# The first two output pairs of a hybrid decoder layer, from a plain and a seven-product multiplication to two interleaved seven-product ones

## Chip, cores and metric

The kernel runs on one core of a Trainium2 chip, as one program. The metric is the device time of one execution in microseconds (us). The kernel before was timed in three runs: median 869.21 us, from 868.64 to 869.86.

## What is computed

The reference is one layer of a hybrid decoder over 2048 rows of width 1024, with 16 learned rows ahead of them, in float32:

```python
hn = rms_norm(h, norm_g)
proj = jnp.einsum('bld,de->ble', hn, w_in)              # 1024 -> 8 groups of 512
cx, cb, cc, cg, q, k, v, rg = jnp.split(proj, N_PROJ, axis=-1)
conv_out = short_conv_branch(cx, cb, cc, conv_w) * jax.nn.silu(cg)
ret_out = head_group_norm(retention_chunkwise(rotary(q), rotary(k), v), g) * jax.nn.silu(rg)
mixed = jnp.concatenate([conv_out, ret_out], axis=-1)
h = h + jnp.einsum('ble,ed->bld', mixed, w_out)         # the output projection
return rms_norm(h, final_g)
```

The change is in the last product, `mixed @ w_out`, a 2048 x 1024 by 1024 x 1024 multiplication, and in the sum and the norm behind it.

## The kernel before

**Numbers in two parts.** Every float32 operand of a large product is split into a high part, which ScalarE (ACT) casts to the matmul type, and a low part, which VectorE (DVE) makes as the operand less its high part (`split`, L112 and L113). One 128 x 512 piece of a product is then three matmuls: low by high, high by low, high by high. On the weight side (stationary) the two parts are the tiles `wh` and `wl`, on the moving side `mh` and `ml`. The stationary tiles live in a ring of three (RING), the moving ones of a whole matrix stay in SBUF: `mh20` to `mh23` are the four 128-row pieces of moving operand 2.

**Seven products.** A 2 x 2 product of blocks is done in seven block products in place of eight, with sums of blocks as operands (Winograd's form). On the stationary side GpSimd (POOL) makes the sums for each pair (`stationary`, four additions and subtractions of 128 x 512). The moving side has seven operands, m0 to m6, four blocks or sums of blocks each. A block product is 12 matmuls (four pieces by three), so seven products are 84 matmuls; `quad` (L236) issues them, with a ScalarE copy of some PSUM banks, and `take` adds up the results. `quad_plain` (L293) does the eight plain products in 96 matmuls, from four stationary parts that it keeps as moving-type tiles, and needs m0, m1, m5 and a plain fourth block m7 alone.

**Stages.** The sequence is done in two halves of 1024 rows; in each half eight units (four retention heads, four convolution groups) project, mix and store 128 columns of `mixed` to DRAM. Behind them the output stage takes `mixed` back in eight pairs of 128-row tiles (`output`, pairs 0 to 7): load four `ra` tiles of `mixed`, multiply by w_out, add the rows of `x` (the `yo` tiles), square and sum on ScalarE, normalise, store. The sums of w_out blocks (m2, m3, m4 and m6, that is `SUMS`) were made in earlier units and lie in DRAM (`sums_w`); those of m3 and m4 are loaded ahead during the last convolution group into the tiles `held`, the others come through the tiles `t`.

**The first pair before.** Pair 0 runs plain, so that it needs no sums; while it runs, m2 and m6, and then m3 and m4, are split. Pairs 1 to 7 run in seven products. In pair 1 the addition of a copied bank to `yo` is on VectorE, in the later pairs on GpSimd.

**What sets the order.** The program is written in Python order, but a scheduler places instructions on each engine by its own estimate of readiness. Each engine then runs its row of instructions strictly in that order: an instruction whose operand is late holds all behind it. All loads and stores named here are issued by SyncE's queue (SP).

## Time and profile before

| | us |
|---|---|
| median of three runs | 869.21 |
| the profiled execution, whole | 868.33 |
| its span, on which the times of the trace are counted | 866.5 |
| TensorE (PE) busy in the span | 855.4 |
| VectorE busy | 725.7 |
| ScalarE busy | 497.8 |
| GpSimd busy | 394.6 |

The trace counts from the start of the span. In it the last convolution group's fifth block product is issued until 697.85 us, the first matmul of the output stage starts at 697.85, and TensorE's last matmul is over some seven us before the span's end. A matmul's duration in a row (0.39 us) is longer than its share of the engine, since matmuls overlap; what one costs is the distance between starts. In a row of the timeline the columns are start, duration, engine, line, operation, tiles and count, and in brackets the idle time ahead and what ended it.

### The profile page before, as it was taken

The numbers are of one execution on the slowest core, as the hardware profiler recorded it, in microseconds if no ns is written. First come the engines' busy times: TensorE is split into PE (matmuls) and PEld (weight loads), VectorE is DVE, ScalarE is ACT, GpSimd is POOL, SyncE is SP. The second block draws the span as 40 slices with busy tenths as digits, with TensorE's granted clock in tenths as the row PEclk, the third lists the DMA queues.
The fourth block names the chain that finished last, engine by engine and source line by source line (L and its number), as shares of the span: only waits on it lengthen the run. The fifth ranks groups of instructions, "written<-read, shape, count | busy, mean of one in ns | idle before, by whom it ended". The sixth has DMA issues, their size and how long they took to land.

```text
span 866.5 us, 12699 instructions
## 1 busy us (share of the span) xinstructions
PE 855.4 (99%) x4216; PEld 705.1 (81%) x4216; DVE 725.7 (84%) x1194; ACT 497.8 (57%) x899; POOL 394.6 (46%) x286
## 2 busy tenths in 40 slices
PE   9999999999999999999999999999999999999996
PEld 6778888888787778788888888888888888788885
DVE  7899988888988977989789898988767799877663
ACT  8676548384755554948374757544333566545553
POOL 0662332423145554352242323354746555677773
PEclk9999999999999999999999999999999999999999
DMA  9724235454656633845264845646123584555431
GB/s 339 233 79 89 72 85 154 113 149 135 159 169 190 199 98 98 313 149 146 62 158 121 159 134 124 205 113 216 48 78 81 173 326 136 169 165 178 156 134 73
DMA packets 127218, 129.51 MB, mean 149 GB/s; under 512 B 58352, under 2 KB 75568, under 8 KB 127152
## 3 DMA queue, kind: packets, MB, share of 16 engines
q1 hardware_dynamic: 126576, 128.30, 50.0%
q8 instruction: 33, 0.54, 0.3%
q10 hardware_dynamic: 576, 0.40, 0.1%
q14 instruction: 33, 0.27, 0.1%
HBM read 90.91 MB, written 25.17 MB: 134 GB/s over the span
## 4 chain that ended last, share of the span: by engine, by line
PE 78%; DVE 6%; issue 1%; ACT 0%; POOL 0%; POOLq 0%; DVEq 0%
PE pj L236 66%; PE pj L293 5%; PE ms L831 1%; PE ms L820 1%; PE ms L830 1%; PE ms L807 1%; DVE wl L113 1%; PE ms L456 1%; DVE ml L113 1%; DVE ml L116 0%; DVE yo L121 0%; DVE yo L906 0%; DVE yo L941 0%; ACT n L407 0%; DVE tc L121 0%
## 5 line engine op out<-in xcount | busy, mean ns | idle before, releaser
L236 PE MATMUL pj<-mh,wl 128*128 128x512 f32 x1008 | 396.0, 393 | 1.3 <-DVE wl L113 0.7
L236 PE MATMUL pj<-mh,wh 128*128 128x512 f32 x1008 | 393.1, 390 | 0.0
L236 PE MATMUL pj<-ml,wh 128*128 128x512 f32 x1008 | 392.9, 390 | 0.0
L112 ACT CAST wh<-ra 128x512 fp32r<-128x512 f32 x216 | 133.9, 620 | 232.1 <-PE pj L236 193.6
L236 PEld LDWEIGHTS pj<-mh,wl 128*128 128x128 f32 x1008 | 189.3, 188 | 43.1 <-issue 1.5
L113 DVE TENSOR_TENSOR wl<-ra,wh 128x512 fp32r<-128x512 f32 x216 | 192.4, 893 | 36.6 <-ACT wh L112 35.2
L236 PEld LDWEIGHTS pj<-mh,wh 128*128 128x128 f32 x1008 | 189.3, 188 | 39.4
L236 PEld LDWEIGHTS pj<-ml,wh 128*128 128x128 f32 x1008 | 189.3, 188 | 38.1
L121 POOL TENSOR_TENSOR sa<-ra 128x512 f32<-128x512 f32 x36 | 54.1, 1504 | 108.8 <-DMA ra<-in_w_in 50.5
L124 POOL TENSOR_TENSOR ra<-sa,ra 128x512 f32<-128x512 f32 x36 | 51.3, 1424 | 81.8 <-DVE wl L113 79.6
L124 POOL TENSOR_TENSOR ra<-ra 128x512 f32<-128x512 f32 x36 | 59.1, 1641 | 59.2 <-PE ms L456 48.9
L151 POOL TENSOR_TENSOR ra<-ra 128x512 f32<-128x512 f32 x36 | 61.5, 1709 | 47.3 <-issue 35.2
L243 ACT COPY tc<-pj 128x512 f32<-128x512 f32 x108 | 62.6, 580 | 0.1
L293 PE MATMUL pj<-mh,mh 128*128 128x512 f32 x128 | 51.0, 401 | 0.6 <-ACT mh L115 0.6
L293 PE MATMUL pj<-mh,ml 128*128 128x512 f32 x128 | 50.0, 390 | 1.0 <-DVE ml L113 1.0
L293 PE MATMUL pj<-ml,mh 128*128 128x512 f32 x128 | 48.0, 391 | 0.0
L843 POOL TENSOR_TENSOR rp<-rs,neg_half 128x4 f32<-128x4 f32 x16 | 19.4, 1211 | 46.4 <-DVE rs L121 46.2
L596 POOL TENSOR_TENSOR c<-c,rr 128x512 f32<-128x512 f32 x14 | 25.7, 1834 | 22.2 <-DVE c L637 14.1
L906 DVE TENSOR_TENSOR yo<-pj,yo 128x512 f32<-128x512 f32 (+1 forms) x33 | 22.0, 671 | 15.9 <-PE pj L236 8.5
L917 POOL TENSOR_TENSOR z<-yo,final_g 128x512 f32<-128x512 f32 x16 | 26.8, 1674 | 18.6 <-DVE yo L906 18.6
L847 DVE TENSOR_SCALAR pm<-ms,mv,rp 128x128 f32<-128x128 f32 x64 | 21.9, 403 | 11.8 <-POOL rp L843 11.8
L112 ACT CAST wh<-sa 128x512 fp32r<-128x512 f32 x36 | 22.2, 618 | 16.0 <-PE pj L236 15.8
(153 smaller groups left out, 1223.2 us busy)
## 6 DMA issues: line engine op xcount, KB each, us to landing
ra<-in_w_in SPq DMA_DIRECT2D x126, 256.0 KB, 2.9
x<-in_xT SPq DMA_DIRECT2D x48, 256.0 KB, 5.0
w<-in_w_out SPq DMA_DIRECT2D x32, 256.0 KB, 4.7
ra<-mixed SPq DMA_DIRECT2D x32, 256.0 KB, 2.7
yo<-in_x SPq DMA_DIRECT2D x32, 256.0 KB, 4.6
ra<-in_x SPq DMA_DIRECT2D x16, 256.0 KB, 3.3
mixed<-c SPq DMA_DIRECT2D x16, 256.0 KB, 2.5
sums_x<-x SPq DMA_DIRECT2D x16, 256.0 KB, 2.8
```

The costliest lines, as they stand in the source:

```text
L112: nc.scalar.copy(out=hi, in_=src)
L113: lowered[0] = eng.tensor_tensor(out=lo, in0=src, in1=hi.bitcast(F32), op=ALU.subtract)
L121: eng.tensor_tensor(out=out, in0=a, in1=b, op=ALU.add)
L124: eng.tensor_tensor(out=out, in0=a, in1=b, op=ALU.subtract)
L151: summed[0] = nc.gpsimd.tensor_tensor(out=a12, in0=a12, in1=a11, op=ALU.subtract)
L236: nc.tensor.matmul(bank, a[:, ks], b, start=first and kt == 0 and n == 0, stop=kt == KH - 1 and n == 2, skip_group_check=not first,)
L243: copied[0] = nc.scalar.copy(out=c, in_=bank)
L293: nc.tensor.matmul(banks[i], a[:, ks], b, start=half + kt + n == 0, stop=half == 1 and kt == KH - 1 and n == 2,)
L596: eng.tensor_tensor(out=out, in0=a, in1=b, op=ALU.mult)
L847: nc.vector.tensor_scalar(out=y[:, cs], in0=o[:, cs], scalar1=mv[:, c, 0:1], scalar2=rp[:, c, :], op0=ALU.subtract, op1=ALU.mult,)
L906: last[0] = nc.vector.tensor_tensor(out=y[:, cs], in0=pp[:, cs], in1=y[:, cs], op=ALU.add)
L917: nc.gpsimd.tensor_tensor(out=ys[i][j], in0=y, in1=final_g[:, j * HB : (j + 1) * HB], op=ALU.mult)
```

## The change

The first two pairs no longer run one after the other. A new function `quads` runs them together: product 0 of pair 0, product 0 of pair 1, product 1 of pair 0 and so on, both in seven products, each with two PSUM banks. `stationary_in_turn` is a generator: it makes a pair's seven stationary operands one by one, in the order in which the products use them, with the same four GpSimd operations as `stationary`, but in place, without the tile `sa`; the operand of product 4 is written over that of product 3. `moving_in_turn` splits m0 and m1 first, and m2, m3, m4, m5, m6 between the products, in that order. The plain fourth block m7 is no longer made. The rows of `x` for both pairs are loaded behind the first product, the additions of copied banks to `yo` are all on GpSimd, and the norms of both pairs are written behind the last product.

```diff
-    lowered, fifth = [None], [None]
     def split(hi, lo, src, scale=None, eng=nc.vector):
         if scale is None:
             nc.scalar.copy(out=hi, in_=src)
-            lowered[0] = eng.tensor_tensor(out=lo, in0=src, in1=hi.bitcast(F32), op=ALU.subtract)
+            sub(eng, lo, src, hi.bitcast(F32))
             return
         nc.scalar.mul(hi, src, scale)
         nc.vector.scalar_tensor_tensor(
...
         sub(nc.gpsimd, a21, a11, a21)
         sub(nc.gpsimd, a11, s1, a11)
         summed[0] = nc.gpsimd.tensor_tensor(out=a12, in0=a12, in1=a11, op=ALU.subtract)
-        w += [parts(a) for a in (a11, s1, a21)]
-        fifth[0] = lowered[0]
-        return w + [parts(a) for a in (a12, a22)]
+        return w + [parts(a) for a in (a11, s1, a21, a12, a22)]
+    def stationary_in_turn(blocks):
+        a11, a12, a21, a22 = blocks
+        def parts(src):
+            hi = sb.tile([P, HB], F32R, name="wh", tag="wh", bufs=RING)
+            lo = sb.tile([P, HB], F32R, name="wl", tag="wl", bufs=RING)
+            split(hi, lo, src)
+            return hi, lo
+        yield parts(a11)
+        add(nc.gpsimd, a21, a21, a22)
+        sub(nc.gpsimd, a11, a21, a11)
+        yield parts(a12)
+        sub(nc.gpsimd, a12, a12, a11)
+        yield parts(a11)
+        yield parts(a21)
+        sub(nc.gpsimd, a21, a22, a11)
+        yield parts(a21)
+        yield parts(a12)
+        yield parts(a22)
     def operand(i, kt):
         slot = B12 if i == 7 else i
...
                     parts(m, BLOCK[half][j], kt, blocks[-1], scale(k) if scale else None)
                     after.get((j, k), lambda: None)()
         return m, blocks
+    def moving_in_turn(load, scale, sums):
+        m = [[] for _ in range(8)]
+        def blocks(half, j):
+            for kt in range(KH):
+                k = half * KH + kt
+                parts(m, BLOCK[half][j], kt, load(k, j), scale(k) if scale else None)
+        blocks(0, 0)
+        blocks(1, 0)
+        steps = [
+            lambda: sums(m, 1), lambda: sums(m, 0), lambda: sums(m, 2), lambda: blocks(1, 1), lambda: sums(m, 3),
+        ]
+        return m, steps
     def block_sums(b11, b12, b22, b21, t1, t3, f, g, eng=nc.vector):
...
         take(0, 1, zb, u2)
         product(6, xb, False)
         take(1, 0, xb, None)
...
+    def quads(ws, m, takes, between=()):
+        between = iter(between)
+        banks = [[None, None] for _ in ws]
+        copies = [None for _ in ws]
+        def product(n, i, bank, first):
+            wh, wl = next(ws[n])
+            for kt in range(KH):
+                ks = slice(kt * P, (kt + 1) * P)
+                mh, ml = m[i][kt]
+                for s, (a, b) in enumerate(((wl, mh), (wh, ml), (wh, mh))):
+                    nc.tensor.matmul(
+                        bank, a[:, ks], b, start=first and kt == 0 and s == 0, stop=kt == KH - 1 and s == 2,
+                        skip_group_check=not first,
+                    )
+        def copy(bank):
+            c = sb.tile([P, HB], F32, name="tc", tag="tc", bufs=COPIES)
+            copied[0] = nc.scalar.copy(out=c, in_=bank)
+            return c
+        for i in range(7):
+            for n, take in enumerate(takes):
+                if i < 2:
+                    banks[n][i] = ps_proj()
+                bank = banks[n][1 if i in (1, 3, 5) else 0]
+                product(n, i, bank, i in (0, 1, 3))
+                if i == 0:
+                    copies[n] = copy(bank)
+                elif i == 1:
+                    take(0, 0, bank, copies[n])
+                elif i == 2:
+                    copies[n] = [copy(bank)]
+                elif i == 3:
+                    copies[n].append(copy(bank))
+                elif i == 4:
+                    take(1, 1, bank, copies[n][1])
+                elif i == 5:
+                    take(0, 1, bank, copies[n][0])
+                else:
+                    take(1, 0, bank, None)
+            next(between, idle)()
...
-    def output(pair, m, final_g):
+    def output(pair, final_g):
...
-        for i in range(2):
-            for j in range(2):
-                y = gen("yo")[:, :HB]
-                row = (2 * pair + i) * P
-                nc.sync.dma_start(y, x[row : row + P, j * HB : (j + 1) * HB])
-                ys[i][j] = y
+        def fetch():
...
-                with tc.issue_after(fifth[0].ins) if pair == 1 and i + j == 0 else nullcontext():
-                    add(nc.vector if pair == 1 else nc.gpsimd, y, y, c)
+                add(nc.gpsimd, y, y, c)
...
-                if pair and i + j == 0:
+                if pair > 1 and i + j == 0:
...
-        if pair == 0:
-            w = plain_parts(loads)
-            prepared(m, sums_w, (1, 3))
-            quad_plain(w, m, take)
-            prepared(m, sums_w, (0, 2), held)
-        else:
-            quad(stationary(load_raw(loads)), m, take, (idle, idle, square))
-        for i in range(2):
...
+        def finish():
+            for i in range(2):
...
+        return loads, fetch, take, square, finish
...
-    m, b = moving(load_w_out)
+    m, in_turn = moving_in_turn(load_w_out, None, lambda m, n: prepared(m, sums_w, (n,), held))
     final_g = row_tile("final_g", 1)
     nc.sync.dma_start(final_g, t["final_g"].partition_broadcast(P))
-    for pair in range(SEQ // (2 * P)):
-        output(pair, m, final_g)
+    first_pairs = [output(pair, final_g) for pair in range(2)]
+    def behind_first(sums=in_turn[0]):
+        sums()
+        for _, fetch, *_ in first_pairs:
+            fetch()
+    quads(
+        [stationary_in_turn(load_raw(loads)) for loads, *_ in first_pairs], m, [take for _, _, take, *_ in first_pairs],
+        [behind_first] + in_turn[1:],
+    )
+    for *_, finish in first_pairs:
+        finish()
+    for pair in range(2, SEQ // (2 * P)):
+        loads, fetch, take, square, finish = output(pair, final_g)
+        fetch()
+        quad(stationary(load_raw(loads)), m, take, (idle, idle, square))
+        finish()
```

Up to the last convolution group all five engines have the same rows of instructions as before. The places from which the rows differ are these.

TensorE at the end of the last convolution group, before. `pj` are PSUM banks; L236 is `quad`, L293 `quad_plain`. Product 5 of the convolution (`mh50` by `wl_6911`) stands behind a first part of pair 0:

```order
L293 MATMUL pj_7205<-mh03_7046,mh30_7135 128x512
L293 MATMUL pj_7205<-mh03_7046,ml30_7136 128x512
L293 MATMUL pj_7205<-ml03_7047,mh30_7135 128x512
L293 MATMUL pj_7205<-mh10_7052,mh31_7147 128x512
L236 MATMUL pj_6965<-mh50_3880,wl_6911 128x512
L236 MATMUL pj_6965<-ml50_3881,wh_6910 128x512
L236 MATMUL pj_6965<-mh50_3880,wh_6910 128x512
```

The same engine now, from the end of the convolution's last product on (L272 is `quad`, L320 `quads`):

```order
L272 MATMUL pj_6918<-mh62_3965,wh_6914 128x512
L272 MATMUL pj_6918<-mh63_3971,wl_6915 128x512
L272 MATMUL pj_6918<-ml63_3972,wh_6914 128x512
L272 MATMUL pj_6918<-mh63_3971,wh_6914 128x512
L320 MATMUL pj_7094<-mh00_7028,wl_7096 128x512
L320 MATMUL pj_7094<-ml00_7029,wh_7095 128x512
```

All of the convolution's products now stand ahead of the output stage, whose first matmul needs `wl_7096`, the low part of pair 0's first stationary block.

VectorE at the same place, before. `ml` and `wl` are low parts, `tc` and `c` belong to the convolution's results:

```order
L113 TENSOR_TENSOR wl_6915<-ra_6883,wh_6914 128x512
L121 TENSOR_TENSOR tc_6978<-pj_6918,tc_6978 128x512
L113 TENSOR_TENSOR ml70_7077<-w_7074,mh70_7076 128x512
L113 TENSOR_TENSOR ml71_7083<-w_7080,mh71_7082 128x512
L113 TENSOR_TENSOR ml72_7089<-w_7086,mh72_7088 128x512
L113 TENSOR_TENSOR ml73_7095<-w_7092,mh73_7094 128x512
L637 TENSOR_TENSOR c_6873<-tc_6978,c_6873 128x512
L113 TENSOR_TENSOR ml50_7101<-w_7098,mh50_7100 128x512
L113 TENSOR_TENSOR ml51_7107<-w_7104,mh51_7106 128x512
L113 TENSOR_TENSOR ml33_7154<-ra_7151,mh33_7153 128x512
L121 TENSOR_TENSOR tc_6960<-pj_6965,tc_6960 128x512
```

The same stretch now:

```order
L122 TENSOR_TENSOR ml40_7277<-held_6722,mh40_7276 128x512
L122 TENSOR_TENSOR ml21_7141<-t_7138,mh21_7140 128x512
L718 TENSOR_TENSOR c_6873<-tc_6978,c_6873 128x512
L122 TENSOR_TENSOR ml41_7281<-held_6722,mh41_7280 128x512
L119 TENSOR_TENSOR tc_6960<-pj_6965,tc_6960 128x512
L122 TENSOR_TENSOR ml22_7147<-t_7144,mh22_7146 128x512
L122 TENSOR_TENSOR ml42_7285<-held_6723,mh42_7284 128x512
L122 TENSOR_TENSOR ml23_7153<-t_7150,mh23_7152 128x512
L122 TENSOR_TENSOR wl_7096<-ra_7078,wh_7095 128x512
L122 TENSOR_TENSOR ml43_7289<-held_6723,mh43_7288 128x512
L718 TENSOR_TENSOR c_6869<-pj_6918,c_6869 128x512
L122 TENSOR_TENSOR wl_7115<-ra_7086,wh_7114 128x512
```

The low parts of m2 and m4, from `t` and `held`, stand where those of m7 and m5 stood; `wl_7096` comes behind them in row 900 of VectorE's program, 15 rows behind row 885, the first that differs, and `wl_7115`, pair 1's first operand, three rows later.

GpSimd around the first products of the output stage, before (`sa` and `ra` are the stationary sums of pair 1, `z` the results times the final gain):

```order
L121 TENSOR_TENSOR sa_7390<-ra_7386,ra_7388 128x512
L124 TENSOR_TENSOR ra_7386<-ra_7382,ra_7386 128x512
L596 TENSOR_TENSOR c_6873<-c_6873,tc_6960 128x512
L124 TENSOR_TENSOR ra_7382<-sa_7390,ra_7382 128x512
L151 TENSOR_TENSOR ra_7384<-ra_7384,ra_7382 128x512
L917 TENSOR_TENSOR z_7258<-yo_7125,final_g_7122 128x512
L917 TENSOR_TENSOR z_7319<-yo_7131,final_g_7122 128x512
```

Now:

```order
L119 TENSOR_TENSOR ra_7090<-ra_7090,ra_7092 128x512
L122 TENSOR_TENSOR ra_7078<-ra_7082,ra_7078 128x512
L122 TENSOR_TENSOR ra_7086<-ra_7090,ra_7086 128x512
L122 TENSOR_TENSOR ra_7080<-ra_7080,ra_7078 128x512
L677 TENSOR_TENSOR c_6873<-c_6873,tc_6960 128x512
L119 TENSOR_TENSOR yo_7156<-yo_7156,tc_7111 128x512
L122 TENSOR_TENSOR ra_7088<-ra_7088,ra_7086 128x512
L119 TENSOR_TENSOR yo_7164<-yo_7164,tc_7130 128x512
L1000 TENSOR_TENSOR z_7195<-yo_7156,final_g_7074 128x512
L1000 TENSOR_TENSOR z_7220<-yo_7164,final_g_7074 128x512
L122 TENSOR_TENSOR ra_7082<-ra_7084,ra_7078 128x512
L119 TENSOR_TENSOR yo_7158<-yo_7158,tc_7255 128x512
```

Both pairs' stationary sums and their additions to `yo` alternate there. The second `ra_7082` row, which makes pair 0's operand of product 4, is the eleventh of these. A first sum of pair 0, `ra_7082<-ra_7082,ra_7084`, stands three rows ahead of the first row shown, between two multiplications of the convolution group. In SP's queue the four loads of m6's `t` tiles now come behind five loads of `ra` tiles for pairs 2 and 3.

More of the change, by code (lines that the diff above doesn't have):

```diff
@@ L881, in output @@
         cuts = [1, 1]
[L882 to L887 removed]
+        def fetch():
+            for i in range(2):
+                for j in range(2):
+                    y = gen("yo")[:, :HB]
+                    row = (2 * pair + i) * P
+                    nc.sync.dma_start(y, x[row : row + P, j * HB : (j + 1) * HB])
+                    ys[i][j] = y
         last = [None]
```

37 lines of the change are left out of this document (19 added, 18 removed).

## Prediction

> **What bounds the kernel now.** I read the page first, then the chain of waits, then the stretch around the start of the output stage engine by engine.
>
> ```profile
> span 866.5 us, 12699 instructions
> PE 855.4 (99%) x4216; PEld 705.1 (81%) x4216; DVE 725.7 (84%) x1194; ACT 497.8 (57%) x899; POOL 394.6 (46%) x286
> PE 78%; DVE 6%; issue 1%; ACT 0%; POOL 0%; POOLq 0%; DVEq 0%
> ```
>
> TensorE is busy 99% of the span and carries 78% of the chain, so a matmul less is time less, and a wait of TensorE is time more. What a matmul costs stands in the chain's rows (start, length, work):
>
> ```profile
> 698.01 3.20 PE pj L293 x14
> ...
> 707.56 17.02 PE pj L293 x75
> 724.57 0.46 DVE ml L113
> ...
> 742.05 117.28 PE pj L236 x516
> ```
>
> 17.02 / 75 = 0.227 us in the plain form, 117.28 / 516 = 0.227 in the seven-product form. Between the two the chain runs through VectorE: from 724.57 to 742.05 it is VectorE's row of work that ends last. How far TensorE feels that, the stretches by engine tell (first number after the window: its length; then busy times), and the list of TensorE's waits between 690 and 860 us:
>
> ```profile
> 697.85:703.30 5.45, 5.45 (x25) 4.50 (x24) 5.45 (x10) 3.46 (x7) 3.15 (x1) 1.00 1.05 387
> 703.30:709.00 5.70, 5.70 (x27) 4.71 (x26) 5.70 (x8) 4.37 (x8) 3.17 (x2) 1.00 1.05 386
> ...
> 740.00:745.00 5.00, 4.50 (x20) 3.38 (x19) 4.73 (x7) 1.92 (x5) 2.92 (x2) 1.00 0.67 201
> PE pj L236 <- DVE yo L906: 0.5, 1, 0.5
> ```
>
> TensorE and VectorE are both busy without a hole from 697.85 to 709, and TensorE waits once, 0.5 us, at 742. So at the start of the output stage TensorE is the bound with VectorE right behind it: what VectorE does later than TensorE wants it becomes a wait at once.
>
> **What goes.** Pair 0 takes 84 matmuls in place of 96: 12 x 0.227 = **-2.7 us**. The wait at 742 stands in pair 1's product 6, behind VectorE's additions of copies and results, and VectorE loses three of those additions and one split: **-0.5**. The rest that VectorE is spared lies beside TensorE's work and counts for nothing by itself.
>
> **The wait that comes.** Here is VectorE at the place where the orders part:
>
> ```profile
> 696.15 0.68 DVE L113 TENSOR_TENSOR wl<-ra,wh 128x512 fp32r<-128x512 f32 x1
> 696.75 0.68 DVE L113 TENSOR_TENSOR ml<-w,mh 128x512 fp32r<-128x512 f32 x1
> 697.35 1.88 DVE L113 TENSOR_TENSOR ml<-ra,mh 128x512 fp32r<-128x512 f32 x3
> 699.16 0.68 DVE L113 TENSOR_TENSOR wl<-ra,wh 128x512 fp32r<-128x512 f32 x1
> 699.76 0.68 DVE L121 TENSOR_TENSOR tc<-pj,tc 128x512 f32<-128x512 f32 x1
> 700.36 3.00 DVE L113 TENSOR_TENSOR ml<-w,mh 128x512 fp32r<-128x512 f32 x4
> 703.28 0.68 DVE L637 TENSOR_TENSOR c<-tc,c 128x512 f32<-128x512 f32 x1
> 703.88 2.38 DVE L113 TENSOR_TENSOR ml<-w,mh 128x512 fp32r<-128x512 f32 x2
> ```
>
> No row shows an idle time, and an undisturbed operation takes 0.60 from start to start (697.35 to 699.16 for three) and 0.68 to its end. The row of 697.35 is the first that differs. Before, TensorE had 14 matmuls of pair 0 to do from 698 on (the chain's row of 698.01) and put more between the convolution's products 5 and 6, because pair 0's own operands were the four rows at 697.35 and 700-704. Now TensorE does products 5 and 6 at once: their `wl` rows are those of 696.15 and 699.16, so they can run from 697.85 on, and end at 697.85 + 24 x 0.227 = 703.3. The first matmul of the output stage then needs `wl_7096`, and that is 15 rows behind the row of 697.35: 697.35 + 15 x 0.60 = 706.4, done at 706.4 + 0.68 = 707.1. That is a wait of **3.8 us** even if nothing disturbs VectorE, and it is longer than what the change removes. ScalarE's casts ahead of it are no cover and no limit:
>
> ```profile
> 697.88 2.18 ACT L112 CAST mh<-w 128x512 fp32r<-128x512 f32 x4
> ```
>
> 0.55 each, against VectorE's 0.60. But VectorE is disturbed, by GpSimd:
>
> ```profile
> 688.49 3.57 POOL L596 TENSOR_TENSOR c<-c,rr 128x512 f32<-128x512 f32 x1 [2.02 <-DVE c L521]
> 696.61 4.39 POOL L596 TENSOR_TENSOR c<-c,tc 128x512 f32<-128x512 f32 x1 [4.55 <-ACT tc L622]
> 704.04 1.68 POOL L596 TENSOR_TENSOR c<-c,rr 128x512 f32<-128x512 f32 x1 [3.04 <-DVE c L637]
> 707.50 1.72 POOL L121 TENSOR_TENSOR sa<-ra 128x512 f32<-128x512 f32 x1 [1.79 <-DMA ra<-mixed]
> ...
> 749.77 1.29 POOL L121 TENSOR_TENSOR yo<-yo,tc 128x512 f32<-128x512 f32 x1
> ```
>
> A GpSimd operation takes 1.29 by itself. When the one of 696.61 got through, at about 701, the four VectorE rows from 700.36 took 3.00 for 4 x 0.60, 0.6 more; under the one of 704.04 two rows took 2.38 for 1.20, 1.2 more. Both GpSimd operations are still there in the new order, in the same stretch: 707.1 + 0.6 + 1.2 = 708.9, a wait of 5.6. A third has been put ahead of them (`ra_7082<-ra_7082,ra_7084`) and may cost another 1.2, which makes 6.8. Between 3.8 and 6.8 I take **+6.0**: the two collisions are in the trace, and the third happens or not. Behind the waiting first product stand all 168 matmuls of the two pairs; on VectorE, pair 1's `wl_7115` and the read that frees its bank come three rows after `wl_7096`, 2.4 or 3.0 us with a collision, against 2.7 for the first product, so they add little of their own.
>
> **What the wait does to the clock.** The trace has one long idle time of TensorE, at the very end (the first row, of the chain, is VectorE taking the last result; the last column but two of the windows is the granted clock), and one start from idle:
>
> ```profile
> 859.35 0.76 DVE yo L906 x2
> 861.00:862.00 1.00, 0.00 (x0) 0.00 (x0) 0.26 (x2) 0.00 (x0) 0.55 (x1) 1.00 0.88 334
> 862.00:863.00 1.00, 0.00 (x0) 0.00 (x0) 0.75 (x1) 0.72 (x1) 0.00 (x0) 0.68 0.37 139
> 863.00:864.00 1.00, 0.00 (x0) 0.00 (x0) 0.00 (x0) 0.00 (x0) 0.00 (x0) 0.50 0.38 143
> 0.99 4.45 PE L965 MATMUL ms<-warm 128*128 128x512 bf16 x10 [0.99 <-DVE warm L957]
> 4.87 1.31 PE L293 MATMUL pj<-mh,mh 128*128 128x512 f32 x2
> 6.02 0.40 PE L293 MATMUL pj<-mh,ml 128*128 128x512 f32 x1
> ```
>
> A mean of 0.68 in 862 to 863 puts the fall to 0.50 at 862.36, 3.0 us after the last matmul. The first ten matmuls took 0.44 each, and the pace of 0.23 is there from 6.0 on: some 4 to 5 us at half pace, which lose 2.0 to 2.5. A wait of 6.0 in mid-program is twice 3.0. No row shows such a fall inside the program, so the bounds are 0 and 2.5, and I take **+1.5**. [...]
>
> **Waits inside the two pairs.** Product 4 of pair 0 needs the eleventh of the GpSimd operations that begin with pair 1's sum. They take 11 x 1.29 = 14.2 undisturbed, 11 x 1.72 = 18.9 beside VectorE, and cast and low part another 0.55 + 0.68: 15.4 to 20.1. TensorE wants it 8 products or 96 x 0.227 = 21.8 after its first. That fits by 1.7 to 6.4, but the rows of 688.49 and 696.61 show GpSimd kept out for 2.3 and 3.1 while VectorE worked on without a break; two such cost 4.6 to 6.2, which leaves a wait of up to 4.5. The pieces of m6 come last. Their loads now stand in SP's queue behind five loads of `ra` for later pairs, each of which waits for a buffer, and such a load took long here:
>
> ```profile
> t<-sums_w SPq DMA_DIRECT2D x8, 256.0 KB, 5.4
> ```
>
> They are wanted 12 x 2.7 = 33 us after the first product; a queue that comes free late by a third of a load's 5.4 gives up to 2, else nothing. Both together lie between 0 and 6.5; I take **+1.5**, near the low end, since by the mean durations all fits. Pairs 2 to 7 have the same instructions as before.
>
> **Sum.** -2.7 - 0.5 + 6.0 + 1.5 + 1.5 = **+5.8 us**. The profiled execution took 868.33, 1.8 around its span of 866.5, and would take 874.1; the median of the runs is 0.9 above it, so I predict 869.2 + 5.8 = **875.0 us**.
>
> **The rivals.**
>
> *The wait is hidden and the gain arrives: faster.* Eight loads of w_out fewer go out ahead of the first product, and in the windows above the transfers ran at 387 GB/s, a share of 1.05. If VectorE's rows up to 697.35 waited for loads, they would come earlier now. It decides at `wl_7096` being done by 703.3, 3.8 earlier than in the undisturbed count; the price is -2.7 - 0.5 = -3.2, or 866.0. Against it: VectorE shows no idle time in that stretch, and its rows up to there are the same. 0.06.
>
> *The wait is the bare 3.8*, GpSimd gets through without touching VectorE, the clock holds and the rest fits: +0.6, 869.8, no difference that can be told. Against it are the two collisions at 700 and 704. 0.10.
>
> [...]
>
> *GpSimd becomes the bound of the two pairs*: eleven operations in turn with VectorE's splits, which keep it out as at 696.61. The last term is then 6 in place of 1.5: +10.3, 879.5. 0.17.
>
> That the pairs do not run in turn is no rival: the order on TensorE has them so.
>
> **How the numbers follow.** The forecast proper, with a clock that falls, has 0.47 and its own range 873.5 to 877.5. The range over all cases, 870.5 to 880.0, leaves out the two cases at the low end (0.16) and the tail of GpSimd as the bound. A measurement of this kernel tells 0.2%, 1.7 us, from no change. Faster by more: 0.06, the first rival. Within it: 0.10, the bare wait. Slower: 0.47 + 0.20 + 0.17 = 0.84.
>
> **What would show it.** In the changed kernel's trace: TensorE's rows of the convolution end near 703.3 and `pj<-mh,wl` of the output stage starts between 707 and 710, released by VectorE's `wl`, with VectorE busy all through; the granted clock in the windows right behind is below 1.00 for 3 to 5 us, or it is not; TensorE's waits list VectorE's `wl` or `ml` again some 22 and 33 us later, or not. The step on the new wait is wrong if TensorE goes from the convolution into the output stage without a hole of 3 us. The sum is wrong at its root if the matmuls' distance changes elsewhere in the program, or if the stages ahead of 690 us differ in time.

## The result, and the profile after

The changed kernel takes 878.93 us (median of four runs, 878.10 to 879.16), the kernel before beside it 868.98 (868.64 to 869.86). The ratio is 1.0107, with a 95% interval of 1.0094 to 1.0119: slower, by 9.3 us by the ratio and by 9.95 by the two medians. The profiled execution took 878.8, its span is 877.0.

The top of the page of the changed kernel (busy time by engine, and engines' shares of the chain of waits):

```profile
span 877.0 us, 12677 instructions
PE 856.5 (98%) x4204; PEld 703.9 (80%) x4204; DVE 727.9 (83%) x1190; ACT 498.8 (57%) x901; POOL 406.1 (46%) x296
PE 72%; DVE 7%; issue 3%; DMA 1%; POOL 1%; ACT 1%; SPq 0%; POOLq 0%; DVEq 0%
```

TensorE has 12 matmuls less, 4204 in place of 4216, and TensorE carries less of the chain, 72% in place of 78%. The chain from the convolution's end on (start, length, work):

```profile
708.48 3.34 DVE ml L122 x3
712.48 16.30 PE pj L320 x60
...
738.04 16.36 PE pj L320 x70
767.31 3.40 POOL yo L119 x2
771.48 98.23 PE pj L272 x432
```

98.23 / 432 = 0.227, the old distance, so the matmuls of the later pairs cost what they cost before. 16.30 / 60 = 0.272: the first 60 of the two pairs do not. TensorE's waits between 690 and 860 us (in all, times, longest) are these:

```profile
PE pj L320 <- DVE wl L122: 6.3, 2, 5.1
PE pj L272 <- DVE wl L122: 1.7, 1, 1.7
PE pj L272 <- DVE tc L119: 0.5, 1, 0.5
```

Before, this list had one wait of 0.5. Now it has these four, beside one of 0.3 in pair 2: two inside the convolution's last products (L272, `quad`), and two in `quads` (L320), ahead of the first product and of product 4 of pair 0. The stretches by engine (length, then busy times of TensorE, its loads, VectorE, ScalarE, GpSimd; the last but two is the clock):

```profile
697.85:703.30 5.45, 3.70 (x17) 2.76 (x16) 5.45 (x8) 5.45 (x12) 1.50 (x1) 1.00 1.05 385
709.00:712.00 3.00, 0.00 (x0) 0.00 (x0) 3.00 (x4) 0.00 (x0) 1.67 (x2) 0.79 0.00 0
712.00:715.00 3.00, 2.52 (x6) 2.04 (x7) 3.00 (x5) 0.00 (x0) 1.76 (x2) 0.50 0.12 39
715.00:718.00 3.00, 3.00 (x9) 2.33 (x9) 2.00 (x2) 0.75 (x2) 3.00 (x2) 0.57 0.15 49
```

From 709 to 712 TensorE does nothing while VectorE is busy throughout; then the clock stands at half until about 717.6. Where VectorE was held up shows on its own rows, and on GpSimd's at the same times:

```profile
695.96 4.09 DVE L122 TENSOR_TENSOR ml<-w,mh 128x512 fp32r<-128x512 f32 x3
...
701.18 1.88 DVE L122 TENSOR_TENSOR ml<-held,mh 128x512 fp32r<-128x512 f32 x3
...
709.47 1.74 DVE L122 TENSOR_TENSOR ml<-held,mh 128x512 fp32r<-128x512 f32 x1
711.14 0.68 DVE L122 TENSOR_TENSOR ml<-t,mh 128x512 fp32r<-128x512 f32 x1
711.74 0.68 DVE L122 TENSOR_TENSOR wl<-ra,wh 128x512 fp32r<-128x512 f32 x1
```

```profile
685.84 1.09 POOL L677 TENSOR_TENSOR u<-u,tc 128x512 f32<-128x512 f32 x1
...
695.55 1.65 POOL L119 TENSOR_TENSOR ra<-ra 128x512 f32<-128x512 f32 x1 [3.67 <-DMA ra<-mixed]
698.01 1.50 POOL L677 TENSOR_TENSOR c<-c,tc 128x512 f32<-128x512 f32 x1 [0.81 <-ACT tc L703]
...
708.96 1.70 POOL L119 TENSOR_TENSOR ra<-ra 128x512 f32<-128x512 f32 x1
```

The three splits from 695.96 on take 4.09 in place of 1.88: two GpSimd operations, one of them the first stationary sum of pair 0 that the change put there (695.55), lie beside them and lengthen them by 2.2, or 1.1 each. `wl_7096` is VectorE's row of 711.74.

**The sum.** By TensorE's start-to-start times the last matmul starts 10.4 later than before (869.31 against 858.93). Of that: -2.7 for the 12 matmuls; -0.7 for the old stall at 742; +1.9 and +0.7 in the convolution (at 700.8 and 704.3); +5.3 at the first output matmul (712.48); +2.5 for the 12 matmuls from there on, which take 5.2 in place of 2.72; +1.3 at product 4 of pair 0 (738.04, the 97th matmul of the two pairs); +0.5 at 771.48, in pair 2; together 8.8. Another 1.05 was there before the change begins: the GpSimd row `u<-u,tc` above, at 685.84, stands earlier in the trace of before, though the program up to there is the same:

```profile
684.79 1.09 POOL L596 TENSOR_TENSOR u<-u,tc 128x512 f32<-128x512 f32 x1
```

By so much two traces differ ahead of any change: over all fourteen traces of this document that row lies between 684.53 and 687.40. Where places in two traces are compared closely below, they count from that row. Some 0.5 lie in pieces too small to name.

### The profile page after: what moved, and what is told of

It reads as the page before. It is cut to its first block, busy times and chain, and to the rows that moved or that the text cites. A ratio compares the mean times of both kernels' runs of the same rounds, so it can differ in the third digit from the quotient of the medians.

```text
span 877.0 us, 12677 instructions
## 1 busy us (share of the span) xinstructions
PE 856.5 (98%) x4204; PEld 703.9 (80%) x4204; DVE 727.9 (83%) x1190; ACT 498.8 (57%) x901; POOL 406.1 (46%) x296
## 4 chain that ended last, share of the span: by engine, by line
PE 72%; DVE 7%; issue 3%; DMA 1%; POOL 1%; ACT 1%; SPq 0%; POOLq 0%; DVEq 0%
PE pj L272 59%; PE pj L320 4%; PE pj L374 2%; DVE ml L122 2%; DVE wl L122 1%; PE ms L911 1%; PE ms L912 1%; PE ms L901 1%; PE ms L888 1%; DMA yo<-in_x 1%; PE ms L537 1%; DMA w<-in_w_out 1%; POOL yo L119 0%; DVE qg L941 0%; DVE ml L114 0%
## 5 line engine op out<-in xcount | busy, mean ns | idle before, releaser
L272 PE MATMUL pj<-mh,wl 128*128 128x512 f32 x980 | 385.3, 393 | 3.6 <-DVE wl L122 2.6
L272 PE MATMUL pj<-mh,wh 128*128 128x512 f32 x980 | 382.2, 390 | 0.0
L272 PE MATMUL pj<-ml,wh 128*128 128x512 f32 x980 | 382.0, 390 | 0.0
L122 DVE TENSOR_TENSOR wl<-ra,wh 128x512 fp32r<-128x512 f32 x224 | 203.6, 913 | 40.6 <-ACT wh L110 38.0
L272 PEld LDWEIGHTS pj<-mh,wl 128*128 128x128 f32 x980 | 184.1, 188 | 45.2 <-ACT mh L110 2.1
L272 PEld LDWEIGHTS pj<-mh,wh 128*128 128x128 f32 x980 | 184.0, 188 | 38.4
L272 PEld LDWEIGHTS pj<-ml,wh 128*128 128x128 f32 x980 | 184.1, 188 | 36.8
L122 POOL TENSOR_TENSOR ra<-ra 128x512 f32<-128x512 f32 x41 | 67.2, 1640 | 61.2 <-PE ms L537 48.9
L122 POOL TENSOR_TENSOR ra<-sa,ra 128x512 f32<-128x512 f32 x35 | 49.5, 1415 | 83.1 <-DVE wl L122 80.9
L149 POOL TENSOR_TENSOR ra<-ra 128x512 f32<-128x512 f32 x35 | 60.2, 1721 | 49.5 <-issue 38.3
L374 PE MATMUL pj<-mh,mh 128*128 128x512 f32 x96 | 38.4, 400 | 1.7 <-ACT mh L1087 1.1
L374 PE MATMUL pj<-mh,ml 128*128 128x512 f32 x96 | 37.5, 391 | 0.4 <-DVE ml L122 0.4
L119 POOL TENSOR_TENSOR yo<-yo,tc 128x512 f32<-128x512 f32 x24 | 36.3, 1521 | 3.4 <-ACT tc L279 2.4
L374 PE MATMUL pj<-ml,mh 128*128 128x512 f32 x96 | 35.7, 392 | 0.0
L119 DVE TENSOR_TENSOR tc<-pj,tc 128x512 f32<-128x512 f32 x28 | 19.2, 686 | 14.2 <-PE pj L272 14.0
```

What stands on the lines that cost most here:

```text
L119: eng.tensor_tensor(out=out, in0=a, in1=b, op=ALU.add)
L122: eng.tensor_tensor(out=out, in0=a, in1=b, op=ALU.subtract)
L149: summed[0] = nc.gpsimd.tensor_tensor(out=a12, in0=a12, in1=a11, op=ALU.subtract)
L272: nc.tensor.matmul(bank, a[:, ks], b, start=first and kt == 0 and n == 0, stop=kt == KH - 1 and n == 2, skip_group_check=not first,)
L374: nc.tensor.matmul(banks[i], a[:, ks], b, start=half + kt + n == 0, stop=half == 1 and kt == KH - 1 and n == 2,)
```

## The experiments

Each kernel ran beside the kernel before on the same chip. The level of the kernel before differs by about 1 us between these groups (medians 868.48 to 869.63), so kernels of different rows are compared by their ratio to the kernel before; a thousandth is 0.87 us. "Sums" are GpSimd's eight stationary sums in the two pairs, "adds" its six additions of copied banks to `yo`.

| label | kernel | us | ratio (95%) | TensorE's waits, 690 to 860 us |
|---|---|---|---|---|
| | the change | 878.93 | 1.0107 (1.0094 to 1.0119) | 8.8 |
| e2_busy_wait | change, first wait filled with idle matmuls | 878.41 | 1.0111 (1.0094 to 1.0128) | 5.8 |
| e1_in_time | change, splits of m2 to m4 in time | 876.80 | 1.0094 (1.0077 to 1.0111) | 7.3 |
| e3_sums_later | change, first sums later | 877.32 | 1.0094 (1.0079 to 1.0109) | 8.1 |
| e4_both | both of these | 876.96 | 1.0092 (1.0077 to 1.0107) | 7.8 |
| e5_sums_vector | e4, sums on VectorE | 872.76 | 1.0037 (1.0024 to 1.0050) | 3.9 |
| e6_sums_adds_vector | e4, sums and adds on VectorE | 869.37 | 0.9998 (0.9988 to 1.0007) | 2.5 |
| e7_no_sums | e4, sums left out | 869.13 | 0.9991 (0.9982 to 1.0001) | 1.8 |
| e8_less12 | the kernel before, 12 matmuls left out | 870.05 | 1.0004 (0.9994 to 1.0014) | 2.1 |
| e9_no_gain_product | e6, gain product on VectorE too | 868.77 | 1.0000 (0.9990 to 1.0009) | 2.2 |
| e11_vector_alone | change, sums and adds on VectorE | 873.76 | 1.0055 (1.0041 to 1.0069) | 4.5 |
| e14_pairs_apart | e9, pairs not interleaved | 875.30 | 1.0070 (1.0055 to 1.0085) | 7.3 |
| e15_change_apart | change, pairs not interleaved | 879.92 | 1.0120 (1.0103 to 1.0137) | 8.8 |

In the rows quoted below line numbers are a few off those of the change: L114 or L122 is a low part there, L272 to L277 `quad`, L320 to L325 `quads`.

### Is it the order, or the clock?

**Splits in time.** The splits of m2, m3 and m4 are tied behind pair 1's stationary split of the product before:

```diff
-            nc.scalar.copy(out=hi, in_=src)
-            sub(eng, lo, src, hi.bitcast(F32))
+            parted[:] = [
+                nc.scalar.copy(out=hi, in_=src),
+                eng.tensor_tensor(out=lo, in0=src, in1=hi.bitcast(F32), op=ALU.subtract),
+            ]
...
+    def behind(sums):
+        cast, rest = parted
+        with tc.issue_after(cast.ins), tc.issue_after(rest.ins):
+            sums()
     def behind_first(sums=in_turn[0]):
-        sums()
+        behind(sums)
...
-        [behind_first] + in_turn[1:],
+        [behind_first] + [lambda f=f: behind(f) for f in in_turn[1:3]] + in_turn[3:],
```

> The changed kernel with one thing added: on ScalarE and VectorE the splits of m2, m3 and m4 may each stand only behind pair 1's stationary split of product 0, 1 and 2. Theory (the order on VectorE makes the wait): the 5.3 us wait ahead of the output stage's first matmul goes, and with it the 12 matmuls at half pace (2.3 us): 878.9 - 7.6 = 871.3 us. The wait of 1.9 ahead of the convolution's product 5 stays. Rival (VectorE and GpSimd have too much to do in this stretch, whatever the order): the wait comes back ahead of products 2 to 4, and the time stays at 876 or more.

It took 876.80, as the rival had it. TensorE's first output matmul no longer waits 5.1, and later ones do, here those of products 1 and 2 of pair 0 (TensorE's timeline; in brackets the wait):

```profile
711.54 0.50 PE L324 MATMUL pj<-mh,wl 128*128 128x512 f32 x1 [0.39 <-DVE wl L114]
720.60 0.80 PE L324 MATMUL pj<-mh,wl 128*128 128x512 f32 x1 [3.33 <-DVE wl L114]
```

**The wait filled.** 22 matmuls of the warm-up kind, whose result nobody reads, stand behind the convolution's last matmul, and the first output product behind them:

```diff
+                if i + n == 0:
+                    with tc.issue_after(issued[0].ins):
+                        warm_up(AGAIN)
...
-                product(n, i, bank, i in (0, 1, 3))
+                with tc.issue_after(warmed[0].ins) if i + n == 0 else nullcontext():
+                    product(n, i, bank, i in (0, 1, 3))
```

> The changed kernel with 22 idle matmuls of 512 columns (the ones of the opening, on a bank that nobody reads) between the convolution's last matmul and the output stage's first; at 0.227 each they fill 5.0 of the 5.3 us wait. Theory (the wait halves the clock for 12 matmuls): the first products run at 0.227 again, 2.3 us less: 876.6. Rival (the slow first product is paced by its operands): no gain, 878.9.

It took 878.41, not faster. The half pace behind the first wait is gone, and a longer wait stands at product 4 of pair 0:

```profile
710.62 0.50 PE L321 MATMUL pj<-mh,wl 128*128 128x512 f32 x1 [0.39 <-DVE wl L122]
735.97 0.56 PE L321 MATMUL pj<-mh,wl 128*128 128x512 f32 x1 [3.29 <-DVE wl L122]
```

Behind that wait the matmuls stand 0.43 apart and the clock has a mean of 0.66 from 735 to 740: the half pace has come back there. What is gained ahead of VectorE is lost at the next place where TensorE meets it. What the half pace costs apart from the waits, this run can't tell.

**First sums later.** The first GpSimd sum of each pair stands behind the convolution's last weighting product:

```diff
-        add(nc.gpsimd, a21, a21, a22)
+        with tc.issue_after(weighed[-2].ins):
+            add(nc.gpsimd, a21, a21, a22)
...
-            mul(nc.gpsimd, cs[j], cs[j], c)
+            weighed.append(nc.gpsimd.tensor_tensor(out=cs[j], in0=cs[j], in1=c, op=ALU.mult))
```

> The changed kernel with the first GpSimd sum of each pair put behind the convolution group's product of c and tc on GpSimd. Theory (the third GpSimd operation in the stretch holds up VectorE, and so the convolution's products 5 and 6): the waits of 1.9 and 0.7 us there go, the convolution ends at 703.3 + 1 in place of 707.2, and wl of pair 0 comes about 2 us earlier: 876.9. Rival (the sum only collides with other splits, later): 878.9.

877.32, near the number expected, but its interval overlaps with that of the change, and not all steps came. The two waits in the convolution are gone. Counted from `u<-u,tc`, which stands at 686.83 in this trace, the convolution's last matmul starts 2.5 us earlier than in the change, and `wl_7096` (VectorE's row of 711.58) only 1.15, since the moved sum (GpSimd, 703.01) now holds a split there. The wait before the first output matmul grew to 6.5:

```profile
PE pj L321 <- DVE wl L122: 7.7, 2, 6.5
```

**Both together.** The edits of e1_in_time and of e3_sums_later in one kernel:

> Both of these together: the splits of m2 to m4 in time, and the sums behind the convolution's product on GpSimd. If the two add: 878.9 - 7.6 - 2.0 = 869.3, as fast as the kernel before, with the 12 matmuls saved still paid for by waits of 1.3 and 0.5 us inside the two pairs and about 1 us ahead of 685 us. If VectorE's whole work is the bound, 875 or more.

876.96: the theory that the order of the splits and the early sum alone made the loss falls. Each wait is now short, but there are six, 7.4 us in `quads`. VectorE's row shows why, with GpSimd's of the same time:

```profile
711.07 1.28 DVE L114 TENSOR_TENSOR wl<-ra,wh 128x512 fp32r<-128x512 f32 x2
712.27 6.85 DVE L114 TENSOR_TENSOR ml<-held,mh 128x512 fp32r<-128x512 f32 x4
719.04 1.75 DVE L114 TENSOR_TENSOR wl<-ra,wh 128x512 fp32r<-128x512 f32 x1
```

```profile
711.82 1.67 POOL L126 TENSOR_TENSOR ra<-ra 128x512 f32<-128x512 f32 x1 [1.23 <-DVE wl L114]
713.45 1.72 POOL L123 TENSOR_TENSOR yo<-yo,tc 128x512 f32<-128x512 f32 x1
715.13 1.73 POOL L126 TENSOR_TENSOR ra<-ra 128x512 f32<-128x512 f32 x1
716.83 1.74 POOL L123 TENSOR_TENSOR yo<-yo,tc 128x512 f32<-128x512 f32 x1
```

GpSimd works without a break from 711.82 on, and four splits, 2.4 by themselves, take 6.85: each GpSimd operation holds VectorE for 1.1. Two SBUF inputs stand in every row of VectorE above. Where one input lies in PSUM, no such loss shows: in the changed kernel's trace from 500 us on, 37 single 128 x 512 operations of VectorE with one input in PSUM (`pj`) lie beside a 128 x 512 operation of GpSimd for more than 0.3 us, and each took 0.68 or 0.69; of those with both inputs in SBUF, 76 lie beside one, and they took up to 1.84, against 0.66 to 0.69 for the 78 that lie beside none.

### Is it GpSimd beside VectorE?

The new theory: VectorE's row paces the two pairs, and a GpSimd operation beside it costs VectorE 1.1, while the same operation on VectorE costs 0.60. Then work is to be moved onto the engine that is full. Three kernels, all on top of the last one:

```diff
-            add(nc.gpsimd, a21, a21, a22)
-        sub(nc.gpsimd, a11, a21, a11)
+            add(nc.vector, a21, a21, a22)
+        sub(nc.vector, a11, a21, a11)
```

(and the other two of `stationary_in_turn` likewise)

> Both edits of the last run (GpSimd's first sums later, moving splits in time) stay, and the eight stationary sums of the two pairs go from GpSimd to VectorE. In that run's trace VectorE has no idle time from 695 to 741 us, and every GpSimd operation that runs beside it lengthens a row of VectorE by about 1.1 us (ml<-held x4 takes 6.85 in place of 4 x 0.60 under four GpSimd operations), while the same operation on VectorE takes 0.60. Theory (VectorE with GpSimd's operations in its way bounds the two pairs): each sum moved spares VectorE 0.5, 8 x 0.5 = 4.0, so 877.0 - 4.0 = 873.0 us (872 to 875). Rival (VectorE is full, so work moved onto it comes on top): + 8 x 0.6 = 4.8, 881.8 us.

```diff
-                add(nc.gpsimd, y, y, c)
+                add(nc.vector if pair < 2 else nc.gpsimd, y, y, c)
```

> As the run before, and the six additions of copied banks to yo of these two pairs go to VectorE too, so that GpSimd has fourteen operations fewer beside it. Theory (a GpSimd operation costs VectorE 1.1, the same on VectorE 0.6): 14 x 0.5 = 7.0 less, and no wait long enough to lower the clock, another 1.4 less: 877.0 - 8.4 = 868.6 us (867.5 to 871.5), and VectorE's x4 rows of 6.85 shrink to about 2.4 to 3.5. Rival (work moved onto a full VectorE comes on top): + 14 x 0.6 = 8.4, 885.4 us. Second rival (VectorE's new additions wait for ScalarE's copies and hold the splits behind them): between 871.5 and 877.

```diff
-        with tc.issue_after(weighed[-2].ins):
-            add(nc.gpsimd, a21, a21, a22)
-        sub(nc.gpsimd, a11, a21, a11)
...
-        sub(nc.gpsimd, a12, a12, a11)
...
-        sub(nc.gpsimd, a21, a22, a11)
```

> Both edits of the run with splits in time and later sums stay, and the eight stationary sums of the two pairs are left out: their operands are then single blocks in place of sums of blocks, with as many splits and matmuls as before. Theory (GpSimd's operations lengthen VectorE's by 1.1 each): 8 x 1.1 = 8.8 off VectorE, more than the waits of 7.6 and the 1.4 of half pace can all give, so about 868 us (867 to 870). Rival (the number of splits alone bounds the stretch, GpSimd being beside it): no change, 877 us, within 1 us.

872.76, 869.37 and 869.13: all three by the theory, none by a rival. By the ratios the first gives 0.0055 or 4.8 us for eight operations moved, 0.60 each; the second 0.0094 or 8.2 us for fourteen, 0.58 each; the third 0.0101 or 8.8 us for eight left out, 1.1 each. TensorE's rows are the same in all three as in the kernel they start from; in the third, so are VectorE's and ScalarE's. The stretch from 700 to 742 us in one window each, for the kernel before, for e4_both and for e6_sums_adds_vector (third pair of numbers: VectorE's busy time and operations; fifth: GpSimd's):

```profile
700.00:742.00 42.00, 41.55 (x184) 34.08 (x182) 40.85 (x53) 22.97 (x46) 20.43 (x14) 1.00 0.54 189
```

```profile
700.00:742.00 42.00, 35.20 (x144) 27.37 (x143) 40.62 (x37) 20.71 (x41) 31.52 (x20) 0.96 0.35 115
```

```profile
700.00:742.00 42.00, 39.83 (x172) 31.64 (x171) 39.62 (x59) 26.16 (x52) 15.35 (x10) 1.00 0.51 165
```

VectorE is busy for 40 of 42 us in all three. With 20 GpSimd operations beside it, it gets 37 done, 1.10 each; with 10, it gets 59 done, 0.67 each. Busy time tells nothing here; the count does. VectorE's row in e4_both shows no idle time up to 741 us either, so it isn't that the sums came late. In the change itself VectorE has holes in the same window:

```profile
700.00:742.00 42.00, 34.42 (x137) 27.33 (x138) 32.90 (x40) 18.40 (x36) 26.68 (x17) 0.92 0.34 112
```

There the order of the splits bounds the start, and VectorE is full throughout only once that order is mended. The four splits that took 6.85 now read:

```profile
712.74 2.48 DVE L114 TENSOR_TENSOR ml<-held,mh 128x512 fp32r<-128x512 f32 x4
```

**VectorE alone.** The same move without the other order:

> The changed kernel with one edit alone: the eight stationary sums and the six additions to yo of the first two pairs on VectorE in place of GpSimd; neither the splits nor anything else is put in another order, so pair 0's first low part still stands behind splits of m2, m3 and m4. If the amount of VectorE's work and GpSimd's hold on it were the whole cause, the gain is that of the same edit beside the other order, 7.6: 878.9 - 7.6 = 871.3 us or less. If the order counts by itself once VectorE has room, the wait before the first product stays at 4.5 to 5.3 with 2.3 of half pace, while the waits behind it go: 869.4 + 7 - 2.8 = 873.6 us (872.5 to 875.5), and TensorE's gap stands at about 711. Rival (the sums were not the matter here): 878 us or more.

873.76, as expected if the order counts by itself. Of the four waits of the change one is left, that before the first output matmul, a little shorter than the 4.5 to 5.3 expected and ending at 708.76 in place of about 711:

```profile
PE pj L320 <- DVE wl L122: 4.1, 1, 4.1
```

By the ratios the change costs 9.3 us, the other order alone brings 1.3 (within the noise), the other engine alone 4.5, and both 9.5: each is worth the more when the other is there.

### Were 12 matmuls ever worth 2.7 us?

```diff
                         for n, (a, b) in enumerate(((wh, mh), (wl, mh), (wh, ml))):
+                            if short and half == 1 and kt < 3 and n == 1:
+                                continue
...
-            quad_plain(w, m, take)
+            quad_plain(w, m, take, short=True)
```

The scheduler also put a few rows of pair 0 in another order.

> The kernel before, with 12 of the 96 matmuls of pair 0's plain form left out (low by high, in the second half of the contraction), nothing else: the term of -2.7 alone. Theory: 869.0 - 2.7 = 866.3 us if VectorE keeps up with the earlier end of pair 0; the wait at 742 may grow from 0.66 by as much as is gained. Rival (the gain is eaten there, since VectorE and not TensorE bounds that stretch already before): 868.5 to 869.0 us.

870.05, a ratio of 1.0004: nothing is gained, as the rival had it. TensorE waits once, at 731.27, for a copy on ScalarE:

```profile
PE pj L236 <- ACT tc L243: 2.1, 1, 2.1
```

ScalarE's row, in this kernel:

```profile
728.75 0.63 ACT L915 ACTIVATE rot<-yo 128x512 f32<-128x512 f32 x1 [1.30 <-DVE yo L908]
...
730.64 0.58 ACT L243 COPY tc<-pj 128x512 f32<-128x512 f32 x1
```

The copy stands behind two squares that waited for VectorE's `yo`. Counted from `u<-u,tc` (686.04 here), it starts 44.6 us later, against 44.9 in the kernel before: TensorE came earlier, the copy did not. So in the kernel before it is VectorE, not TensorE, that sets this stretch, and a wait took what the matmuls gave, with half pace behind it, which the stretch from 730 to 735 shows (0.78):

```profile
730.00:735.00 5.00, 3.73 (x12) 3.00 (x13) 4.40 (x9) 3.06 (x7) 3.78 (x4) 0.78 0.22 84
```

### What is left, and what interleaving is worth

```diff
-            if i == j:
+            if i == j and pair > 1:
                 ys[i][j] = gen("z")[:, :HB]
...
-                    if i == j:
+                    if i == j and pair > 1:
                         nc.scalar.mul(y, y, rs)
...
-        [behind_first] + [lambda f=f: behind(f) for f in in_turn[1:3]] + in_turn[3:],
+        [behind_first] + [lambda f=f: behind(f) for f in in_turn[1:5]] + in_turn[5:],
```

> The run with sums and additions on VectorE, and in the first two pairs GpSimd's four products with the final gain (z<-yo,final_g) go too: VectorE's closing operation takes gain and norm at once, as it does already for the other half of each row tile. All moving splits, those of m5 and m6 too, stay behind pair 1's stationary split of the product before. In the run before this one, GpSimd's row of 717.71 (5.20, two operations) lies beside VectorE's rows of 720.56 to 723.4, which are lengthened by about 1.1 twice, and TensorE's waits there are 1.34 at 717.08 and 0.85 at 723.51. Theory (GpSimd beside VectorE is what is left): both waits go but for some tenths, 869.4 - 1.7 = 867.7 us, 0.2% below the kernel before. Rival (what is left is VectorE's own row of splits): 869.4 within 0.5. Second rival: m5's loads and splits, placed otherwise, make a wait of their own: above 870 us.

868.77, a ratio of 1.0000: the first rival. The waits stay at 2.2 although the stretch now has 61 operations of VectorE beside seven of GpSimd:

```profile
700.00:742.00 42.00, 39.82 (x174) 31.96 (x173) 38.95 (x61) 26.37 (x53) 8.40 (x7) 1.00 0.53 172
```

0.64 each is close to the 0.60 of an undisturbed row. What is left is in the main VectorE's own work, and no version here is clearly faster than the kernel before.

The last two run the pairs one after the other, from this kernel and from the change:

```diff
-    quads(
-        [stationary_in_turn(load_raw(loads)) for loads, *_ in first_pairs], m, [take for _, _, take, *_ in first_pairs],
...
+    for n, (loads, _, take, *_) in enumerate(first_pairs):
+        quads(
+            [stationary_in_turn(load_raw(loads))], m, [take],
...
```

> The last kernel of this line (sums, additions and the gain product on VectorE, splits in time), but the two pairs run one after the other, both in seven products: what the interleaving by itself is worth once nothing stands in VectorE's way. All moving splits must then be done within one pair's 84 matmuls, 19 us. By VectorE's order of work and 0.60 per operation from 699.3 us on (tc<-pj in the interleaved run), the low part for pair 0's product 4 is done at 719.6, where TensorE would want it at 716.7 after some 2 us of waits already had: waits of about 5 in pair 0 and none in pair 1, against 2.7 in the interleaved run. Theory (VectorE's row paces the stretch; interleaving spreads its work over 38 us in place of 19): 868.8 + 2.3 = 871.1 us (870 to 873, the clock falls or not). Rival (interleaving is worth nothing, the sum of VectorE's work decides alone): 868.8 within 0.7.

875.30: worse than either number. That this kernel loses 6.1 us by the ratio when its pairs run one after the other is shown; the guess was 2.3. A single wait makes most of it:

```profile
PE pj L325 <- DVE yo L994: 5.3, 1, 5.3
```

Pair 0's product 3 writes the bank of product 1, which VectorE frees with an addition to `yo`, and in VectorE's row that addition stands behind the splits of m5:

```profile
716.15 2.48 DVE L114 TENSOR_TENSOR ml<-w,mh 128x512 fp32r<-128x512 f32 x4
718.56 0.68 DVE L123 TENSOR_TENSOR yo<-yo,tc 128x512 f32<-128x512 f32 x1
719.16 0.68 DVE L994 TENSOR_TENSOR yo<-pj,yo 128x512 f32<-128x512 f32 x1
```

The expectation had only looked at low parts. How much of the 6.1 is interleaving as such, and how much the order that the scheduler chose without it, stays open.

> The changed kernel with the interleaving alone undone: pairs 0 and 1 one after the other, both in seven products, operands still made in order of use. VectorE's low part for the first product still stands behind splits of m2, m3 and m4, so the wait of 5 before the first output product and the 2.3 of half pace stay, and GpSimd's operations for pair 1 come later. Theory (the order of the splits and VectorE's work make the loss, not the interleaving): 878.9 within 1.5. Rival A (interleaving crowded GpSimd's fourteen operations into VectorE's full stretch and is itself to blame): 875 us or less. Rival B (a single pair leaves only 19 us for 28 splits): 882 us or more.

879.92, within the theory's 1.5: in the change itself, interleaving is neither the harm nor a help that can be told (ratio 1.0120 against 1.0107, intervals that overlap).

## Why the prediction was right, and where not

The sign and the range held: 878.9 is within 870.5 to 880.0, and the wait on `wl_7096` behind the later operands' splits came as drawn. But the number was 3.9 low, outside the likeliest case's own 873.5 to 877.5. Step by step:

**The wait before the first output matmul**, +6.0, measured 5.3. The mechanism was right: 15 rows from 701.18 to 711.74, 10.6 us, are 9.0 and two collisions of 0.5 and 1.1. That these are the two sizes counted is partly luck: they belong to `c<-c,rr` (GpSimd, 707.35) and to pair 1's first sum (708.96), while `c<-c,tc`, which the prediction counted, had gone ahead at 698.01. The wait's place was to be 707 to 710 and is 712.48, because both sides were late: VectorE's first row that differs stands at 701.18, not 697.35. Of these 3.8, 1.05 were there before the change begins.

**The step that failed: "so they can run from 697.85 on"**, of the convolution's products 5 and 6. It took VectorE's rows up to 697.35 as settled, since their order is the same. The new GpSimd sum, which the prediction counted as a third collision that "happens or not", does happen, and ahead of that point: what follows on VectorE, the convolution's `wl` among it, is 2.2 late, and TensorE waits 1.9 and 0.7 there. By TensorE's waits that is 2.6 of the 3.9. It is less of the time: e3_sums_later, which moves that sum, has neither wait, but there `wl_7096` comes only 1.15 earlier, and by the ratio the kernel gains 1.1, which the noise could be.

**The clock**, +1.5, measured 2.5: it fell, to half for 12 matmuls. The mechanism was right, the size at the upper bound of 2.5. That the clock holds through a wait of 5 to 6, to which 0.20 of the chances went, no run shows: it fell at the waits of 5.1 in the change, 5.3 in e14_pairs_apart, 4.5 in e15_change_apart and 4.1 in e11_vector_alone. Whether the fall costs anything by itself stays open: e2_busy_wait kept the clock up behind the first wait and took as long, but it has a wait of 3.3 later and half pace behind that one.

**Waits inside the pairs**, +1.5, measured 1.3 at product 4 of pair 0. Size and place were right, the reason was not: the prediction had GpSimd's eleventh operation come late. It was done at 729.88, 7 us before TensorE was through with product 3 of both pairs (736.8), and its cast at 732.98. The low part stood behind the splits of m5, which took 5.70 in place of 2.4 beside three GpSimd operations, the first of them at 731.76:

```profile
728.59 1.29 POOL L122 TENSOR_TENSOR ra<-ra 128x512 f32<-128x512 f32 x1
...
733.39 3.44 POOL L119 TENSOR_TENSOR yo<-yo,tc 128x512 f32<-128x512 f32 x2
```

```profile
731.60 5.78 DVE L122 TENSOR_TENSOR ml<-w,mh 128x512 fp32r<-128x512 f32 x4
737.30 2.97 DVE L122 TENSOR_TENSOR wl<-ra,wh 128x512 fp32r<-128x512 f32 x3
```

The loads of m6 never showed.

**The stall at 742**, -0.5: it went, and 0.5 came back at 771.48 in pair 2, where a VectorE addition waits for GpSimd. Little is left of the term.

**The matmuls**, -2.7: the count is right, and "a matmul less is time less" is wrong in this stretch of the kernel before. e8_less12 took out 12 matmuls, split as much as before, and gained nothing. The page's 99% for TensorE is no proof of a bound where VectorE has no hole either; the prediction saw that ("with VectorE right behind it") and still booked the gain. In the sum it did no harm: the wait was counted against VectorE's row, and behind the first product of the change VectorE has holes.

**The rival of 879.5, GpSimd as the bound**, came nearest in size, but not by its mechanism: it had VectorE keep GpSimd out and product 4 wait 6. In these pairs it is mostly the other way round. GpSimd's operations hold VectorE, 1.1 each, and the runs with the sums and adds moved or left out show that this and the order of the splits make up the loss: with both undone the whole 9.3 is gone. The prediction named three such collisions at the start and none in the 38 us behind it. It could have seen them in the trace of before: the GpSimd row of 749.77, which it reads as 1.29 "by itself", lies beside a VectorE operation that took 1.87 in place of 0.75:

```profile
749.75 1.87 DVE L941 SCALAR_TENSOR_TENSOR yo<-yo,rf,final_g 128x512 f32<-128x512 f32 x1 [0.66 <-POOL rf L309]
```

That the whole range held is in part luck, since its upper end stood there for this rival.

## What to carry to other kernels

Where VectorE has no idle time, price every GpSimd operation beside it at what it takes from VectorE, not at nothing: here 1.1 us each against 0.60 for the same work on VectorE itself, so that moving work onto the full engine saved 8 us once the order was mended. Count an engine's finished operations per window, since its busy time reads 40 of 42 us whether it gets 37 or 59 done. And before a wait is removed, ask where its engine is met next: filling it, reordering ahead of it and taking 12 matmuls away each only moved the wait.

## What was not expected of the hardware

In these traces the half pace lasts 3.4 us or twice that. In the change it is at half from 710.74 to 717.58 (worked out from the means 0.79 and 0.57 in the windows above): 6.84 us, twice 3.42. In e4_both a wait of only 1.8 (TensorE idle from 710.0 to 711.80) is followed by this (the clock is the last number but two):

```profile
711.80:713.00 1.20, 1.20 (x5) 1.02 (x6) 1.20 (x2) 0.01 (x1) 1.18 (x1) 0.99 0.90 239
713.00:716.30 3.30, 3.30 (x9) 2.56 (x9) 3.30 (x3) 0.00 (x0) 3.30 (x3) 0.50 0.92 317
716.30:718.00 1.70, 1.70 (x9) 1.42 (x8) 1.70 (x2) 1.10 (x3) 1.70 (x2) 0.97 0.03 11
```

Half pace from 712.98 to 716.40, 3.42 again, and 1.2 us after the work had started anew, while three waits of 1.3 to 1.7 later in the same kernel left the clock at 1.00. Worked out in the same way, the half pace lasts 3.4 us in e2_busy_wait, e8_less12 and e11_vector_alone, 6.8 in e1_in_time and e14_pairs_apart, and 6.9 in e15_change_apart. What sets these lengths, and which waits bring the clock down, no run here shows.
